# A hybrid attention and pooling block: TensorE keeps to the order of the program's text from attention on

## The chip, the cores and the metric

The kernel runs on one core of a Trainium2 chip. The metric is device time in microseconds (us); three runs of the kernel before gave 1914.45, 1915.05 and 1915.29 us, median 1915.05. The core's engines each work through an instruction stream of their own and wait for each other by semaphores: TensorE (PE) multiplies matrices and transposes, VectorE (DVE), ScalarE (ACT) and GpSimd (POOL) work elementwise, SyncE (SP) issues the transfers. Only PE writes matmul results to PSUM, from which DVE and ACT read them.

## The reference

One layer over 4096 tokens of width 1024, in float32; cut to what matters:

```python
h    = rms_norm(x, norm_g) * (1 + scale) + shift          # scale, shift, gate from c @ w_ada
proj = h @ w_in                                           # 1024 -> 3*512 + 512 + 1024
q = rms_norm(proj[..., :512]  as 8 heads of 64, q_norm_g)
k = rms_norm(proj[..., 512:1024] as 8 heads, k_norm_g)
v, u, z = the rest
# each chunk of 64 tokens attends to itself and 8 chunks to its left
s = einsum('bqhd,bkhd->bhqk', qn, kn) * 64**-0.5 + bias
a_out = einsum('bhqk,bkhd->bqhd', softmax(s), vn)
p_out = (trailing means of u over 2, 4, 8, 16 tokens - u) @ w_pool * pool_scale
y = concat([a_out, p_out]) * silu(z)
x = x + gate * (y @ w_out)
```

## The kernel before

Each product is made of three passes with split operands (high by high, high by low, low by high), so projections come in threes of matmuls (L599 to L601, and likewise L528 to L530, L863 to L865).

The kernel has three stages. The first (to 557 us) normalises x and makes z and u; its matmuls are L330 to L332. The second, attention, is the one that changes first. It runs in two phases `ph` of four heads; in each phase, eight groups `sg` of 512 tokens. A *unit* is one head of one group, 64 units in all, numbered 0 to 63. For one unit:

- Scores: `s1_items`, four steps of 128 queries. Matmuls L697 and L698 write `sps`, of which there is one buffer. DVE (L702) adds the bias and takes the maximum, ACT (L715) takes the exponential and the row sums, into `p`.
- Transposes and values: `s2_items`. For each key block `tr(j)` transposes up to four 128x128 pieces of `p` on PE (L745) into `ptps` (three buffers), ACT casts them (L751, `pth`) and DVE takes the rest (L752, `ptl`); `pv(j)` multiplies both with v (L763, L764) into `ops`. `tr` runs one key block ahead of `pv`. At the end `fin` adds the two halves (ACT L778, DVE L779), and after every second head POOL multiplies the result by the gate and by the reciprocal sums (L781, L782).
- Work beside it: the projection of one 128-token block to q, k and v for a later group (`proj_items`, 24 wide matmuls for q and k, then 24 narrow ones for v), or, in units 58 to 62, the first part of the output projection (`o_items`).

q and k of a block must be normalised before they are transposed. When the wide matmuls of a block end, ACT copies the result (L612), POOL squares it (L614), DVE sums (L621); after every second block a reciprocal root is taken for the two together (L94 to L102: thirteen small operations on POOL and two on DVE), and POOL scales both blocks (L630). The low part of each half of the next h blocks (L111, `bhl`) is made on POOL, too. `tq` then transposes the four blocks of a group (L651), and the copies (L659 to L671) put them where the scores read them.

In the text, unit u is written as one merged list: `merge` spreads the transposes and values of unit u, the scores of unit u+1 and the projection matmuls evenly over the unit. `turns` inserts the q and k transposes of group g into units 4g-2 (two tiles), 4g-1 and 4g, three places into the list of projection work. The block that a group needs last, 4g+3, is projected in unit 4g-3.

That text is not the order that runs. The program is built with a scheduler that plays the program on a simulated timeline and gives each engine whichever instruction is ready first by it. So projection matmuls are moved forward past transposes whose input is late in that timeline. The third stage (`d_items`, from 1695 us) is the rest of the output projection.

Of the kernel before, what the change touches and what calls it, by code (L numbers as in the profile page):

```python
# [23 lines left out]
KT = D // P  # L24
# [27 lines left out]
def block_kernel(ctx, tc, x, xT, par, crow, w_adaT, w_in, w_uT, bias, w_pool, w_out, rcnt, out):  # L52
    nc = tc.nc
# [422 lines left out]
                    load_wqkv(0, 1, lambda: a_stage(), nc.vector)  # L476


    op = ctx.enter_context(tc.tile_pool(name="b_qk", bufs=9))
    WO = {}  # L480

# [37 lines left out]
    def o_items(i):  # L519
        half, p = osteps[i]  # L520

        def one(k):
            if half == 0 and k == 0:
                XP[p] = (pp.tile([P, SG], F32, name="ps"), load_xr(p, 0))
            ps, xr = XP[p]
            a_, l_ = OH[i]
            wh, wl = WO[10 * half][k]
            nc.tensor.matmul(ps, a_[:, k, :], wh, start=half == 0 and k == 0, stop=False, skip_group_check=True)  # L528
            nc.tensor.matmul(ps, a_[:, k, :], wl, start=False, stop=False, skip_group_check=True)
            nc.tensor.matmul(ps, l_[:, k, :], wh, start=False, stop=k == 3, skip_group_check=True)  # L530
            if k == 3:
                OH.pop(i)
                o_load(i + 2)
                o_done(i)
                if half == 0:
                    t = op.tile([P, 512], F32, name="qkr")
                    nc.scalar.copy(t, ps)
                    nc.sync.dma_start(s1_d[p], t)
                else:
                    nc.vector.tensor_tensor(xr, ps, xr, op=ALU.add)  # L540
                    nc.sync.dma_start(out[p * P : (p + 1) * P, 0:512], xr)
                    XP.pop(p)

        return [lambda k=k: one(k) for k in range(4)]

    with ExitStack() as cb:
# [42 lines left out]
        def proj_items(ph, b, after=None):  # L589
# [3 lines left out]
            def chunk(c, k):  # L593
                if k == 0:
                    hold[c] = pp.tile([P, SG], F32, name="ps")
                ps = hold[c][:, 0:512] if c == 0 else hold[c][:, 0:256]
                a_, l_ = hq[(ph, b), k]
                wh, wl = WB[ph, c, k]
                nc.tensor.matmul(ps, a_, wh, start=k == 0, stop=False)  # L599
                nc.tensor.matmul(ps, a_, wl, start=False, stop=False)  # L600
                nc.tensor.matmul(ps, l_, wh, start=False, stop=k == KT - 1)  # L601
                if k == KT - 1:
                    if c == 0:
                        evac_qk(ps)
                    else:
                        evac_v(ps)
                if c == 1 and k in (3, 7) and after is not None:
                    load_h(*after, k // 4, nc.vector if ph == 0 and b < 5 else None)
# [37 lines left out]
        def tq_items(ph, sg):  # L646
            def tq(which, pair):
                ps = ptp.tile([P, SG], F32, name="ptps")
                c0 = which * 256 + pair * P
                for i in range(NB):  # L650
                    nc.tensor.transpose(  # L651
                        out=ps[:, i * P : (i + 1) * P], in_=QK[ph, sg * NB + i][:, c0 : c0 + P], identity=ident
                    )
                for e in range(2):
# [24 lines left out]
        def s1_items(ph, sg, h):  # L679
            def one(i):  # L680
# [13 lines left out]
                ks = ring[h]  # L694
                for pos, k0, n in parts:
                    o = ps[:, pos : pos + n]
                    nc.tensor.matmul(o, QS[ph, sg, h][:, qc], ks[:, k0 : k0 + n], start=True, stop=False)  # L697
                    nc.tensor.matmul(o, QL[ph, sg, h][:, qc], ks[:, k0 : k0 + n], start=False, stop=True)  # L698
                w0 = 0 if sg > 0 else 512 - i * P
                p_ = sp.tile([P, WIN], F32, name="p")  # L700
                mx = st.tile([P, 1], F32, name="mx")
# [32 lines left out]
        def s2_items(ph, sg, h):  # L734
# [5 lines left out]
            def tr(j):  # L740
                ilo, ihi = max(j, 0), min(j + 4, 3)
                ps = ptp.tile([P, SG], F32, name="ptps")
                for i in range(ilo, ihi + 1):
                    w = (j - i + 4) * P
                    nc.tensor.transpose(  # L745
                        out=ps[:, i * P : (i + 1) * P], in_=Pt[ph, sg, h, i][:, w : w + P], identity=ident
                    )
                r = slice(ilo * P, (ihi + 1) * P)
                a_ = wk.tile([P, SG], F32R, name="pth", bufs=3)
                l_ = wk.tile([P, SG], F32R, name="ptl", bufs=3)  # L750
                nc.scalar.copy(a_[:, r], ps[:, r])  # L751
                nc.vector.tensor_tensor(l_[:, r], ps[:, r], a_[:, r].bitcast(F32), op=ALU.subtract)  # L752
                pts[j] = (a_, l_, r)

            def pv(n):
# [4 lines left out]
                a_, l_, r = pts.pop(j)  # L760
                v = Vt[ph, sg * NB + j][:, pr, e, :]
                last = n == len(js) - 1
                nc.tensor.matmul(o[:, r], v, a_[:, r], start=n == 0, stop=False, skip_group_check=True)  # L763
                nc.tensor.matmul(o[:, r], v, l_[:, r], start=False, stop=last, skip_group_check=True)  # L764
                if last:
                    fin(o)

# [76 lines left out]
        def d_items(i):  # L844
            t, p = steps[i]

            def one(k):
# [12 lines left out]
                a_, l_ = DH[t, p]  # L860
                wh, wl = WO[11 if t == 0 else t][k]
                start = t in (1, 2) and k == 0
                nc.tensor.matmul(ps, a_[:, k, :], wh, start=start, stop=False, skip_group_check=True)  # L863
                nc.tensor.matmul(ps, a_[:, k, :], wl, start=False, stop=False, skip_group_check=True)  # L864
                nc.tensor.matmul(ps, l_[:, k, :], wh, start=False, stop=k == 3, skip_group_check=True)  # L865
                if k < 3:
                    return

# [156 lines left out]
```

## Time and profile before

| | us |
|---|---|
| median of three runs | 1915.05 |
| the profiled execution | 1916.19 |
| its span | 1914.3 |
| busy in it: PE | 1876.1 (98%) |
| DVE | 1198.1 (63%) |
| ACT | 914.9 (48%) |
| POOL | 697.7 (36%) |

Busy time is what an engine's instructions cover. Matmuls are pipelined and the ends of their records are modelled and overlap the next record, so short waits hide in a busy PE; the distance from one start to the next shows them. The chain that ended last is PE for 90%.

### The profile page before, as it was taken

How to read it: one execution, taken by the hardware profiler on the slowest of the kernel's cores; microseconds unless marked ns; L12 is line 12 of the kernel's file. 1: busy time of each engine (PE TensorE's matmuls, PEld its weight loads, DVE VectorE, ACT ScalarE, POOL GpSimd, SP SyncE). 2: the span in 40 equal slices, each digit the busy share in tenths (PEclk: the TensorE clock that was granted, in tenths of full speed). 3: DMA queues.
4: the chain of work that ended last, by engine and by line, in shares of the span. 5: the costliest groups of instructions: out<-in, count | busy, mean ns of one | idle time of the engine just before them, and what ended most of it. 6: DMA issues, size and time to landing. Idle time of an engine off the chain costs nothing.

```text
span 1914.3 us, 29736 instructions
## 1 busy us (share of the span) xinstructions
PE 1876.1 (98%) x10284; PEld 1616.1 (84%) x10284; DVE 1198.1 (63%) x2424; ACT 914.9 (48%) x1951; POOL 697.7 (36%) x966
## 2 busy tenths in 40 slices
PE   8999999999999999999999999999999999989999
PEld 7888888888888888888887888988988888878887
DVE  8676666575544457656656665576566555478875
ACT  5422223332324457656657665576566666432221
POOL 0421355244135553444454564534444433200000
PEclk8999999999999999999999999999999999999999
DMA  9566466567222222221223222222212457686662
GB/s 376 192 198 198 151 216 213 185 200 258 75 100 73 72 67 67 65 69 53 60 83 111 78 85 75 69 61 67 67 62 67 181 185 230 234 297 221 208 205 78
DMA packets 196727, 265.63 MB, mean 139 GB/s; under 512 B 21984, under 2 KB 98272, under 8 KB 196576
## 3 DMA queue, kind: packets, MB, share of 16 engines
q1 hardware_dynamic: 196576, 263.73, 42.1%
q8 instruction: 81, 1.33, 0.3%
q14 instruction: 70, 0.57, 0.1%
HBM read 177.54 MB, written 77.74 MB: 133 GB/s over the span
## 4 chain that ended last, share of the span: by engine, by line
PE 90%; DVE 4%; ACT 2%; DMA 2%; issue 1%; SPq 0%; POOL 0%; ACTq 0%; DVEq 0%; POOLq 0%
PE ps L599 9%; PE ps L600 9%; PE ps L601 9%; PE ptps L745 6%; PE aps L330 5%; PE aps L332 5%; PE aps L331 5%; PE ps L330 4%; PE ps L331 4%; PE ps L332 4%; PE sps L697 3%; PE ops L764 3%; PE sps L698 3%; PE ops L763 3%; PE ptps L865 2%; PE ptps L864 2%
## 5 line engine op out<-in xcount | busy, mean ns | idle before, releaser
L599 PE MATMUL ps<-w,bhh 128*128 128x512 f32 (+1 forms) x1024 | 353.9, 346 | 0.8 <-ACT bhh L110 0.8
L600 PE MATMUL ps<-w,bhh 128*128 128x512 f32 (+1 forms) x1024 | 352.3, 344 | 0.4 <-DVE w L111 0.4
L601 PE MATMUL ps<-w,bhl 128*128 128x512 f32 (+1 forms) x1024 | 351.0, 343 | 0.0
L752 DVE TENSOR_TENSOR ptl<-ptps,pth 128x512 fp32r<-128x512 f32 x480 | 223.4, 485 | 157.3 <-ACT pth L751 153.0
L702 DVE CUSTOM_DVE_ANT_0 p<-sps,nb 128x640 f32<-128x640 f32 (+4 forms) x256 | 199.0, 777 | 127.6 <-PE sps L698 126.5
L751 ACT CAST pth<-ptps 128x512 fp32r<-128x512 f32 x480 | 192.5, 425 | 147.1 <-PE ptps L745 123.1
L111 POOL TENSOR_TENSOR bhl<-bhr,bhh 128x512 fp32r<-128x512 f32 x148 | 190.8, 1292 | 157.7 <-ACT bhh L110 123.4
L715 ACT ACTIVATE p<-p,mx 128x640 f32<-128x640 f32 (+4 forms) x256 | 204.5, 799 | 91.0 <-DVE mx L702 88.5
L745 PE MATMUL ptps<-ident,p 128*128 128x128 f32 x1200 | 215.3, 275 | 1.6 <-ACT p L715 1.4
L599 PEld LDWEIGHTS ps<-w,bhh 128*128 128x128 f32 x1024 | 194.2, 190 | 19.0 <-DVE v L111 1.1
L600 PEld LDWEIGHTS ps<-w,bhh 128*128 128x128 f32 x1024 | 194.1, 190 | 18.5 <-DVE w L111 1.1
L601 PEld LDWEIGHTS ps<-w,bhl 128*128 128x128 f32 x1024 | 194.1, 190 | 16.4
L763 PE MATMUL ops<-pth,v 128*128 128x512 f32 x480 | 162.3, 339 | 5.7 <-ACT pth L751 3.5
L745 PEld LDWEIGHTS ptps<-ident,p 128*128 128x128 f32 x1200 | 147.4, 140 | 21.0 <-ACT p L715 1.9
L697 PE MATMUL sps<-kr,qs 128*128 128x320 f32 (+2 forms) x480 | 154.5, 330 | 8.8 <-DVE mx L702 7.3
L764 PE MATMUL ops<-ptl,v 128*128 128x512 f32 x480 | 154.2, 331 | 2.9 <-DVE ptl L752 2.2
L614 POOL TENSOR_TENSOR sq<-qkr 128x512 f32<-128x512 f32 x64 | 66.6, 1041 | 247.1 <-ACT qkr L612 238.6
L331 PE MATMUL aps<-hlo,w 128*128 128x512 f32 x392 | 152.8, 390 | 0.0
L332 PE MATMUL aps<-hhi,w 128*128 128x512 f32 x392 | 152.8, 390 | 0.0
L330 PE MATMUL aps<-hhi,w 128*128 128x512 f32 x392 | 149.6, 392 | 0.0
L698 PE MATMUL sps<-kr,ql 128*128 128x320 f32 (+2 forms) x480 | 147.3, 317 | 0.0
L331 PE MATMUL ps<-hlo,w 128*128 128x512 f32 x376 | 146.6, 390 | 0.0
(202 smaller groups left out, 3932.0 us busy)
## 6 DMA issues: line engine op xcount, KB each, us to landing
bhr<-hT_d SPq DMA_DIRECT2D x128, 256.0 KB
xt<-in_x_dram SPq DMA_DIRECT2D x32, 512.0 KB
qkr<-in_x_dram SPq DMA_DIRECT2D x64, 256.0 KB
out_dram<-qkr SPq DMA_DIRECT2D x64, 256.0 KB
yv<-yT_d SPq DMA_DIRECT2D x61, 256.0 KB
xt<-in_xT_dram SPq DMA_DIRECT2D x28, 512.0 KB
hT_d<-xt SPq DMA_DIRECT2D x56, 256.0 KB
w<-wg_d SPq DMA_DIRECT2D x20, 512.0 KB
```

What stands on the lines that cost most here:

```text
L330: nc.tensor.matmul(ps, wh[:, cs], a_, start=k == 0, stop=False)
L331: nc.tensor.matmul(ps, wh[:, cs], l_, start=False, stop=False)
L332: nc.tensor.matmul(ps, wl[:, cs], a_, start=False, stop=k == KT - 1)
L599: nc.tensor.matmul(ps, a_, wh, start=k == 0, stop=False)
L600: nc.tensor.matmul(ps, a_, wl, start=False, stop=False)
L601: nc.tensor.matmul(ps, l_, wh, start=False, stop=k == KT - 1)
L697: nc.tensor.matmul(o, QS[ph, sg, h][:, qc], ks[:, k0 : k0 + n], start=True, stop=False)
L698: nc.tensor.matmul(o, QL[ph, sg, h][:, qc], ks[:, k0 : k0 + n], start=False, stop=True)
L745: nc.tensor.transpose(out=ps[:, i * P : (i + 1) * P], in_=Pt[ph, sg, h, i][:, w : w + P], identity=ident)
L752: nc.vector.tensor_tensor(l_[:, r], ps[:, r], a_[:, r].bitcast(F32), op=ALU.subtract)
L763: nc.tensor.matmul(o[:, r], v, a_[:, r], start=n == 0, stop=False, skip_group_check=True)
L764: nc.tensor.matmul(o[:, r], v, l_[:, r], start=False, stop=last, skip_group_check=True)
```

## The change

Two helpers wrap every matmul and transpose from attention on. `keep_in_program_order` ties an instruction to the one before it in the text on the same engine, without a semaphore: the scheduler can't move it ahead. The 2465 PE instructions of the first stage stand as before. No operation, operand or buffer changes; the order of the other engines is chosen by the scheduler again, around PE's new order.

```diff
+    def mm(*a, **kw):
+        tc.keep_in_program_order(nc.tensor.matmul(*a, **kw))
+
+    def turn_(**kw):
+        tc.keep_in_program_order(nc.tensor.transpose(**kw))
...
-                nc.tensor.matmul(ps, a_, wh, start=k == 0, stop=False)
-                nc.tensor.matmul(ps, a_, wl, start=False, stop=False)
-                nc.tensor.matmul(ps, l_, wh, start=False, stop=k == KT - 1)
+                mm(ps, a_, wh, start=k == 0, stop=False)
+                mm(ps, a_, wl, start=False, stop=False)
+                mm(ps, l_, wh, start=False, stop=k == KT - 1)
...
-                    nc.tensor.transpose(
+                    turn_(
                         out=ps[:, i * P : (i + 1) * P], in_=QK[ph, sg * NB + i][:, c0 : c0 + P], identity=ident
                     )
...
-                    nc.tensor.matmul(o, QS[ph, sg, h][:, qc], ks[:, k0 : k0 + n], start=True, stop=False)
-                    nc.tensor.matmul(o, QL[ph, sg, h][:, qc], ks[:, k0 : k0 + n], start=False, stop=True)
+                    mm(o, QS[ph, sg, h][:, qc], ks[:, k0 : k0 + n], start=True, stop=False)
+                    mm(o, QL[ph, sg, h][:, qc], ks[:, k0 : k0 + n], start=False, stop=True)
...
-                nc.tensor.transpose(
+                turn_(
                     out=ps[:, i * P : (i + 1) * P], in_=Pt[ph, sg, h, i][:, w : w + P], identity=ident
                 )
...
-                nc.tensor.matmul(o[:, r], v, a_[:, r], start=n == 0, stop=False, skip_group_check=True)
-                nc.tensor.matmul(o[:, r], v, l_[:, r], start=False, stop=last, skip_group_check=True)
+                mm(o[:, r], v, a_[:, r], start=n == 0, stop=False, skip_group_check=True)
+                mm(o[:, r], v, l_[:, r], start=False, stop=last, skip_group_check=True)
```

`o_items` and `d_items` change likewise. Since the helpers record the instructions, all these matmuls now have line L481 and all transposes L484; tiles tell them apart (`sps` scores, `ptps<-ident,p` transposes of p, `ops` values, `ptps<-ident,qkr` transposes of q and k, `ps` projections). Below L478 the lines move down by 7: L614 becomes L621, L630 L637, L781 and L782 become L788 and L789.

First place: PE, the end of a unit and the start of the next, just ahead of the transposes of group 3. Before:

```order
L697 MATMUL sps<-kr_4826,qs_6818 128x512
L698 MATMUL sps<-kr_4826,ql_4830 128x512
L697 MATMUL sps<-kr_4826,qs_6818 128x128
L698 MATMUL sps<-kr_4826,ql_4830 128x128
L599 MATMUL ps<-w,bhh 128x256
L600 MATMUL ps<-w,bhh 128x256
L601 MATMUL ps<-w,bhl 128x256
L599 MATMUL ps<-w,bhh 128x512
L600 MATMUL ps<-w,bhh 128x512
L764 MATMUL ops<-ptl,v 128x256
L745 MATMUL ptps<-ident,p 128x128
```

Now:

```order
L481 MATMUL sps<-kr_4825,ql_4829 128x512
L481 MATMUL ps<-w,bhh 128x256 x2
L481 MATMUL ps<-w,bhl 128x256
L481 MATMUL ops<-pth,v 128x256
L481 MATMUL ops<-ptl,v 128x256
L481 MATMUL ps<-w,bhh 128x256 x2
L481 MATMUL ps<-w,bhl 128x256
L481 MATMUL ops<-pth,v 128x128
L481 MATMUL ops<-ptl,v 128x128
L481 MATMUL ps<-w,bhh 128x512 x2
L481 MATMUL ps<-w,bhl 128x512
L484 MATMUL ptps<-ident,p 128x128 x4
```

The last of the four transposes reads what the scores at the top give through DVE and ACT. Between them stand now always the same few matmuls; before, the scheduler set them apart as it liked, and cut triples and tiles open.

Second place: PE, the first q and k transposes of group 3, a dozen rows on. Before:

```order
L745 MATMUL ptps<-ident,p 128x128 x2
L764 MATMUL ops<-ptl,v 128x128
L745 MATMUL ptps<-ident,p 128x128 x2
L651 MATMUL ptps<-ident,qkr 128x128 x4
L601 MATMUL ps<-w,bhl 128x512
L599 MATMUL ps<-w,bhh 128x512
```

Now:

```order
L481 MATMUL sps<-kr_4826,qs_6818 128x128
L481 MATMUL sps<-kr_4826,ql_4830 128x128
L481 MATMUL ps<-w,bhh 128x512 x2
L481 MATMUL ps<-w,bhl 128x512
L481 MATMUL ops<-pth,v 128x512
L481 MATMUL ops<-ptl,v 128x512
L484 MATMUL ptps<-ident,qkr 128x128 x4
L484 MATMUL ptps<-ident,p 128x128 x3
```

What the rows don't show is where the block that they need last was projected: now between the wide matmuls of block 15 and these four stand 24 narrow and 9 wide projection matmuls with their share of attention; before, the wide matmuls of blocks 15, 16 and on had been moved ahead by several units.

Third place: POOL, the end of the chain from the square of a block's q and k to the scaling of the pair (here block 11, the last of group 2). Before:

```order
L99 TENSOR_TENSOR rqw<-rqy 128x16
L100 TENSOR_TENSOR rqw<-rqw,rqv 128x16
L101 TENSOR_SCALAR rqw<-rqw 128x16
L102 TENSOR_TENSOR rqy<-rqw,rqy 128x16
L630 TENSOR_TENSOR qkr<-qkr,rqy 128x512 x2
L614 TENSOR_TENSOR sq<-qkr 128x512
L111 TENSOR_TENSOR bhl<-bhr,bhh 128x512 x2
L781 TENSOR_TENSOR osum<-osum,gzb 128x512
L782 TENSOR_TENSOR osum<-osum,rlx 128x512
```

Now:

```order
L111 TENSOR_TENSOR bhl<-bhr,bhh 128x512
L101 TENSOR_SCALAR rqw<-rqw 128x16
L102 TENSOR_TENSOR rqy<-rqw,rqy 128x16
L99 TENSOR_TENSOR rqw<-rqy 128x16
L100 TENSOR_TENSOR rqw<-rqw,rqv 128x16
L788 TENSOR_TENSOR osum<-osum,gzb 128x512
L101 TENSOR_SCALAR rqw<-rqw 128x16
L789 TENSOR_TENSOR osum<-osum,rlx 128x512
L102 TENSOR_TENSOR rqy<-rqw,rqy 128x16
L637 TENSOR_TENSOR qkr<-qkr,rqy 128x512 x2
```

The two multiplications of a finished pair of heads (`osum`) stood behind the scaling of q and k and stand now inside the chain to it; two `bhl` are in the chain before and now (of the two, the last is the first row here). That is so in every group's last block but the first's.

## Rows read from the trace of the kernel before

**Rows 1.** The page: span and busy times.
```profile
span 1914.3 us, 29736 instructions
PE 1876.1 (98%) x10284; PEld 1616.1 (84%) x10284; DVE 1198.1 (63%) x2424; ACT 914.9 (48%) x1951; POOL 697.7 (36%) x966
```
**Rows 2.** Windows: stretch; busy (instructions) by engine; granted clock, DMA share, GB/s.
```profile
700.00:750.00 50.00, 46.95 (x292) 40.27 (x291) 35.69 (x88) 35.58 (x84) 17.28 (x29) 1.00 0.18 54
1000.00:1050.00 50.00, 45.35 (x285) 39.09 (x285) 35.16 (x83) 37.39 (x87) 25.88 (x34) 1.00 0.35 107
1704.70:1708.10 3.40, 1.05 (x5) 0.57 (x4) 3.40 (x7) 0.00 (x0) 0.00 (x0) 1.00 1.05 358
1708.10:1711.50 3.40, 3.40 (x9) 2.62 (x9) 3.04 (x6) 0.00 (x0) 0.00 (x0) 0.50 1.04 353
1750.00:1800.00 50.00, 50.00 (x222) 41.43 (x221) 39.49 (x63) 11.22 (x18) 0.00 (x0) 1.00 0.71 231
556.90:1695.50 1138.60, 1115.98 (x6871) 985.07 (x6871) 679.05 (x1583) 687.89 (x1568) 517.72 (x793) 1.00 0.31 100
```
**Rows 3.** Lines by form, PE, 556.9 to 1695.5: count, busy, mean ns, idle before.
```profile
L745 PE MATMUL ptps<-ident,p 128*128 128x128 f32 x1200 | 215.3, 275 | 1.6 <-ACT p L715 1.4
L599 PE MATMUL ps<-w,bhh 128*128 128x512 f32 x512 | 205.6, 402 | 0.8 <-ACT bhh L110 0.8
...
L599 PE MATMUL ps<-w,bhh 128*128 128x256 f32 x512 | 148.3, 290 | 0.0
L697 PE MATMUL sps<-kr,qs 128*128 128x320 f32 x256 | 81.8, 327 | 4.5 <-DVE mx L702 3.5
```
**Rows 4.** Timeline of PE near 802 us: start, duration, instruction.
```profile
801.38 0.28 PE L601 MATMUL ps<-w,bhl 128*128 128x256 f32 x1
801.50 0.34 PE L763 MATMUL ops<-pth,v 128*128 128x384 f32 x1
...
802.66 0.38 PE L745 MATMUL ptps<-ident,p 128*128 128x128 f32 x2
...
803.00 0.28 PE L601 MATMUL ps<-w,bhl 128*128 128x256 f32 x1
```
**Rows 5.** Timeline, block 19: last wide matmul, square and scaling on POOL.
```profile
797.34 0.48 PE L601 MATMUL ps<-w,bhl 128*128 128x512 f32 x1
...
798.62 1.04 POOL L614 TENSOR_TENSOR sq<-qkr 128x512 f32<-128x512 f32 x1 [3.56 <-ACT qkr L612]
...
807.90 2.04 POOL L630 TENSOR_TENSOR qkr<-qkr,rqy 128x512 f32<-128x512 f32 x2
```
**Rows 6.** Timeline of POOL, block 3, with nothing else in the chain.
```profile
588.88 1.04 POOL L614 TENSOR_TENSOR sq<-qkr 128x512 f32<-128x512 f32 x1 [6.63 <-ACT qkr L612]
...
596.21 2.05 POOL L630 TENSOR_TENSOR qkr<-qkr,rqy 128x512 f32<-128x512 f32 x2
```
**Rows 7.** Lines by form, POOL, attention.
```profile
L781 POOL TENSOR_TENSOR osum<-osum,gzb 128x512 f32<-128x512 f32 x32 | 41.5, 1296 | 125.4 <-DVE osum L779 120.6 <-PE ps L529 2.8 <-issue 1.7
```
**Rows 8.** Timeline near 1686 us: scores, exponential, and the transpose that waits for it.
```profile
1684.80 0.31 PE L698 MATMUL sps<-kr,ql 128*128 128x320 f32 x1
...
1686.50 0.83 ACT L715 ACTIVATE p<-p,mx 128x640 f32<-128x640 f32 x1
...
1687.47 0.44 PE L745 MATMUL ptps<-ident,p 128*128 128x128 f32 x2 [1.19 <-ACT p L715]
```
**Rows 9.** Lines by form, attention: DVE's and ACT's steps of scores and transposes.
```profile
L702 DVE CUSTOM_DVE_ANT_0 p<-sps,nb 128x640 f32<-128x640 f32 x224 | 183.5, 819 | 109.5 <-PE sps L698 108.6
L752 DVE TENSOR_TENSOR ptl<-ptps,pth 128x512 fp32r<-128x512 f32 x120 | 79.4, 683 | 40.7 <-ACT pth L751 39.8
...
L751 ACT CAST pth<-ptps 128x512 fp32r<-128x512 f32 x120 | 66.3, 586 | 34.5 <-PE ptps L745 33.0 <-PE ops L764 0.3
```
**Rows 10.** Timeline of PE: two waits.
```profile
1653.88 0.51 PE L528 MATMUL ps<-w,bhh 128*128 128x512 f32 x1 [1.97 <-ACT bhh L110]
...
1707.59 0.50 PE L863 MATMUL ps<-w,bhh 128*128 128x512 f32 x1 [2.35 <-DVE qkr L870]
```

More of the change, by code (lines that the diff above doesn't have):

```diff
@@ L527, in one @@
             wh, wl = WO[10 * half][k]
-            nc.tensor.matmul(ps, a_[:, k, :], wh, start=half == 0 and k == 0, stop=False, skip_group_check=True)
-            nc.tensor.matmul(ps, a_[:, k, :], wl, start=False, stop=False, skip_group_check=True)
-            nc.tensor.matmul(ps, l_[:, k, :], wh, start=False, stop=k == 3, skip_group_check=True)
+            mm(ps, a_[:, k, :], wh, start=half == 0 and k == 0, stop=False, skip_group_check=True)
+            mm(ps, a_[:, k, :], wl, start=False, stop=False, skip_group_check=True)
+            mm(ps, l_[:, k, :], wh, start=False, stop=k == 3, skip_group_check=True)
             if k == 3:
@@ L862, in one @@
                 start = t in (1, 2) and k == 0
-                nc.tensor.matmul(ps, a_[:, k, :], wh, start=start, stop=False, skip_group_check=True)
-                nc.tensor.matmul(ps, a_[:, k, :], wl, start=False, stop=False, skip_group_check=True)
-                nc.tensor.matmul(ps, l_[:, k, :], wh, start=False, stop=k == 3, skip_group_check=True)
+                mm(ps, a_[:, k, :], wh, start=start, stop=False, skip_group_check=True)
+                mm(ps, a_[:, k, :], wl, start=False, stop=False, skip_group_check=True)
+                mm(ps, l_[:, k, :], wh, start=False, stop=k == 3, skip_group_check=True)
                 if k < 3:
```

## The prediction

> **What bounds the kernel now.** I read the page first: PE is busy for 98% of the span [rows 1], DVE, ACT and POOL for 63, 48 and 36%, so on the face of it PE sets the time and has 38 us to give. That is too small, since the records of matmuls overlap. So I went on to the timeline of PE, for the distance from one start to the next where nothing waits. In the last stage 222 matmuls of 512 columns start in 50 us [rows 2], 0.225 us each. One of 256 columns is followed after 0.12 us; two transposes and one such matmul fill 802.66 to 803.00, so a transpose takes (0.34 - 0.12)/2 = 0.11 [rows 4]. On the straight line through the two sizes, 384, 320 and 128 columns take 0.173, 0.146 and 0.068.
>
> Then the counts, by form, for the attention stretch of 1138.6 us with its 6871 PE instructions [rows 2, 3]. Of 512 columns: 3 x 512 in the projection, 240 in the values (two for each of 120 tiles [rows 9]), 112 in the scores, 384 in the output projection and 38 at the end, 2310 x 0.225 = 520 us. Of 256: 3 x 512 + 240 + 112 = 1888 x 0.12 = 227. Of 320: 2 x 256 = 512 x 0.146 = 75. Of 384 and 128: 352 each, 61 and 24. Transposes: 1200 of p and 256 of q and k, 160. Together 1067 us. So PE loses **72 us** in attention, most of it in pieces too small to be called idle; the windows from 700 and from 1000 us, where only 46.95 and 45.35 us of 50 are covered, are two of the worse stretches [rows 2]. In the first PE has little projection left to run, because the order of before spent it early; the second lies between the phases. 72 us is what a better order could give at most, and the text's order changes only where the losses lie.
>
> **The change, part by part.** No operation is added or removed, so the 1067 us stay; what I work out is the waits in the text's order, each as a time that a result needs less the PE work that now stands in between. Where the next reader is PE itself, everything queued behind it on PE waits along, that is the whole kernel.
>
> *Transposes of q and k (groups 1 to 15).* From the end of block 4g+3's wide matmuls to the fourth q and k transpose stand 24 narrow (2.88 us) and 9 wide projection matmuls (2.03), 15 transposes (1.65), 12 score matmuls (1.75) and 12 value matmuls of all sizes (1.55): 9.9 us. Taken from the modelled end of the last wide matmul it is 9.7, as the record ends 0.16 later than its step. In that time ACT and POOL must copy, square, take the root and scale. In block 19 this ran from 797.82 to 809.94: 12.1 us [rows 5], with two `bhl` inside. With nothing else inside, in block 3, it took 9.4 from the square on (598.26 - 588.88) [rows 6], and with the 0.8 ahead of the square in block 19 (797.82 to 798.62) 10.2. The new order of POOL puts the two `osum` multiplications into it as well, 2 x 1.30 us [rows 7]: 14.7. They will hardly wait themselves: by the same prices the unit's values end 5.4 us after the wide matmuls, copy and addition are done by about 8, and POOL reaches them at 8 to 9. Before PE arrives, it has itself waited about 1.0 us for scores and transposes (next paragraphs). So 14.7 - 10.7 = 4.0 us for each of eleven groups, 44 us. Groups 1 and 9 lie behind shorter units (first transposed pieces only), 7.6 + 1.0 us: 6.1 each, 12. Group 7 has four more splits of new weights in the chain (17.3 - 8.6 = 8.7), group 15 stands at 9.6 (5.1), group 0 has the short chain against 8.8 (1.4). Sum **71 us**. Bounds: without `osum` in the chain and with PE late by 1 us it is 12.1 - 10.7 = 1.4 a group, 30 us in all with the special ones; if the copies or the splits queue for two more us, 100. I take 71, since the order says what is in the chain and rows have each duration.
>
> Before, this wait costs nothing: no row of PE names POOL's scaling, because the wide matmuls of that block ran 28 us of PE work or more ahead.
>
> *Scores to the first transposes of the next unit.* From the last score to the transpose of its piece stand six narrow matmuls (0.72), in every second unit three wide ones as well (0.68), four value matmuls (0.38) and three transposes (0.33): 1.43 and 2.1 us by turns. What it takes, once: the scores' last matmul starts at 1684.80 and is through 0.15 later, ACT's exponential follows at 1686.50, the transpose starts at 1687.47: 2.5 us [rows 8]. The floor, with no queue, is 0.2 to DVE, 0.82 + 0.08 there [rows 9], 0.83 and 0.19 on ACT and 0.1 between them: some 2.05, an estimate from these rows. With 2.5: 1.1 and 0.4 by turns, 0.75 on the mean, for 48 ordinary units 36 us, 0.7 for the eight units of each phase's first group and a bit for the first: **43 us**. At the floor only the odd half waits, 0.6 x 28 = 18; with a mean of 2.8, 60.
>
> *Transposes to values.* ACT's cast and DVE's rest of a full tile take 0.59 + 0.68 [rows 9], 1.6 us with handing over, against 2.4 to 3.4 us of PE work; the last two tiles of a unit, smaller, have 1.1 and 0.9 against 2.0 and 1.6. All are covered unless an exponential or a scaling is in front (0.7 to 0.8 us), as it sometimes will be with DVE 60% and ACT 60% busy (679 and 688 of 1139 us [rows 2]). I take half a collision of 0.8 us per unit: 48 x 0.4 = **19 us**, between 0 and 40.
>
> *The clock.* Behind a wait of 1.97 us at 1651.9 the granted clock stayed at full rate; behind one of 2.35 us at 1705.2 [rows 10] it was 0.50 for the next 3.4 us, 1.2 of 2.4 GHz [rows 2], and nine matmuls started where fifteen fit: 1.4 us lost. A wait of 4 us is longer than either. I take 15 groups x 1.4 with four in five struck, **17 us**; between 0 and 35, as a long wait might cost twice.
>
> *Between the phases, and the end.* Units 26 and 27 have no projection until the second phase's weights are there. Before, the window from 1000 us holds most of that loss; now those units run bare, with the transposes' full 1.6 us against about 1: 10 us. The last unit has the same lack, 5 us. **15 us**, between 10 and 25. The start of the last stage stays as it is.
>
> **Sum.** 71 + 43 + 19 + 17 + 15 = 165 in place of 72: +93 us. The profiled execution took 1916.2 us (its span of 1914.3 and 1.9 around it), which gives 2009; it lies 1.1 above the median of the runs, so **2008 us**.
>
> **The rivals.**
> 1. *The text's even spread pays.* The bare stretches of before fill up, and PE loses only the 15 us between phases and at the end: 1915 - 72 + 15 = 1858. The place is the q and k transposes: it decides from the point where POOL's chain fits into 9.7 us. For it speaks that the distances from transposes to values are all longer than the unqueued times; against it that even the chain without any neighbour took 10.2 [rows 5, 6]. 5%.
> 2. *As much lost as before.* All waits lie at their floors, 30 + 18 + 0 + 0 + 20 = 68: 1911 to 1915. It needs POOL to be done with `osum` beforehand, and empty queues. 4%.
> 3. *Short waits take the clock, too.* Behind the wait of 2.35 us it fell [rows 2, 10]; if each unit's wait for its exponential did the same, 56 x 1.4 = 78 us would come on top, 2086 us. Against it: the window from 700 us has the most waits of its neighbourhood and was granted 1.00 [rows 2]. 6%. The Trainium skill says in "TensorE: Matmul & The Clock Gate", section "A second HAM failure mode: psum-queue depth-cycling", that frequent micro-idles between groups of matmuls made the clock swing between half and full rate. By that rule the time would be this rival's; the trace has not shown it for waits up to 1.97 us.
> 4. *The pins don't bind.* Then nothing moves, 1915. The order of PE shows otherwise: triples stand together from the first matmul of attention to the last. Under 1%.
>
> **How the numbers follow.** Slower by several per cent, as summed: 83%; rival 1 5%, rival 2 4%, rival 3 6%, something else slower 2%. The likeliest is the sum, 2008. Its own range follows from the bounds: the four terms of 30 to 100, 18 to 60, 0 to 40 and 0 to 35 are not at one end all together; half of their joint spread is some 45 us either way, 1963 to 2053. With rivals 1 and 2 below and 3 above left out, 1960 to 2056 holds about 8 in 10. A measurement of this kernel can tell 0.2% (4 us) from no change: slower 92%, within it 2%, faster 6%.
>
> **What would show it.** In the profile after: PE's waits at the transposes of q and k (`ptps<-ident,qkr`) name POOL's `qkr` scaling, some fifteen times with 3 to 5 us each, and the chain of waits goes over POOL; transposes of p wait for ACT's `p` in most units, near 1 us in every second; short stretches at granted clock 0.50 lie behind the long waits; PE's busy share falls to about 93%, with the first stage to 557 us unchanged. I am wrong if POOL's scaling is seldom named, if the waits of the q and k transposes sum to under 30 us, or if the rest of PE's waits alone make up more than 100.

## The result and the profile after

The changed kernel took 2036.94 us (median of 4 runs, 2034.40 to 2040.01), against 1915.17 for the kernel before beside it: a ratio of 1.0635, 95% interval 1.0622 to 1.0649. Forecast were 2008 us, between 1960 and 2056. The profiled execution took 2040.01 us. Its page, span and busy times:

```profile
span 2038.2 us, 29831 instructions
PE 1911.2 (94%) x10284; PEld 1632.9 (80%) x10284; DVE 1218.1 (60%) x2424; ACT 916.5 (45%) x1951; POOL 695.8 (34%) x966
```

Against [rows 1] the span is 124 us longer and POOL's and ACT's work the same to 2 us (DVE's is 20 longer for as many instructions): nothing was added, PE stands still longer. The windows (columns as in [rows 2]):

```profile
1050.00:1100.00 50.00, 33.52 (x196) 28.49 (x195) 26.25 (x59) 28.80 (x64) 23.89 (x31) 0.86 0.35 102
557.90:1817.90 1260.00, 1148.16 (x6869) 999.20 (x6867) 700.56 (x1582) 689.04 (x1567) 514.59 (x793) 0.98 0.29 90
```

All of the difference lies in attention: 1260 us in place of 1138.6 [rows 2], for the same 6870 instructions. The place between the phases, one of the worse stretches before, is now the worst of attention: only 33.52 of 50 us are covered. The granted clock is no longer 1.00 throughout.

The waits of PE by what ended them (us in all, times, the longest):

```profile
PE ptps L484 <- POOL qkr L637: 53.2, 32, 9.0
PE ptps L484 <- ACT p L722: 27.9, 31, 1.4
PE ops L481 <- DVE ptl L759: 12.7, 31, 1.5
PE ps L481 <- DVE qkr L547: 10.1, 12, 1.5
```

The first is the one that no row of before had: two waits in each of 16 groups, for POOL's scaling of q and k. The first two of a group's transposes read a pair of blocks that was scaled earlier; the third and the fourth read the last pair. Here is one of them, group 4, which needs block 19 (as [rows 5]); the timeline of PE and POOL from the last wide matmul of that block:

```profile
849.00 0.39 PE L481 MATMUL ps<-w,bhl 128*128 128x512 f32 x1
...
858.31 1.30 POOL L788 TENSOR_TENSOR osum<-osum,gzb 128x512 f32<-128x512 f32 x1
...
859.74 1.27 POOL L789 TENSOR_TENSOR osum<-osum,rlx 128x512 f32<-128x512 f32 x1
...
861.27 2.04 POOL L637 TENSOR_TENSOR qkr<-qkr,rqy 128x512 f32<-128x512 f32 x2
```

```profile
859.99 0.38 PE L484 MATMUL ptps<-ident,qkr 128*128 128x128 f32 x2
862.37 0.33 PE L484 MATMUL ptps<-ident,qkr 128*128 128x128 f32 x1 [1.99 <-POOL qkr L637]
863.37 0.33 PE L484 MATMUL ptps<-ident,qkr 128*128 128x128 f32 x1 [0.67 <-POOL qkr L637]
```

From the end of the wide matmuls (849.39) to the end of the scaling (863.31) it is 13.9 us, with both `osum` multiplications inside. PE has its first two transposes at 859.99, 10.6 after, and then starts the third 2.4 and the fourth 3.4 us after that. Behind it, windows around two such places, groups 4 and 3:

```profile
860.70:864.10 3.40, 1.06 (x7) 0.83 (x8) 0.00 (x0) 0.50 (x3) 2.53 (x4) 1.00 0.48 149
864.10:867.50 3.40, 3.40 (x11) 2.63 (x10) 1.97 (x3) 1.36 (x3) 0.00 (x0) 0.51 0.28 66
793.00:796.40 3.40, 3.40 (x18) 2.87 (x19) 2.04 (x4) 2.10 (x4) 0.00 (x0) 1.00 0.19 43
```

After group 4 PE ran at 1.2 GHz for 3.4 us; after group 3, where the two waits were 1.24 and 0.67, it stayed at 2.4.

**The account.** For all kernels I took the start of each PE instruction in attention and subtracted, from the distance to the one before, what this pair of shapes takes where nothing waits (close to the prediction's prices [rows 2, 4]; the kernel before comes to 69.9 us by it, not 72). What is left is lost time, put down to the instruction that started late; the total also holds the many steps that are late by less than 0.04. The last column is the length of the stretches at 1.2 GHz in attention.

| | time | q, k transposes | p transposes | values | scores and projections | total lost | at 1.2 GHz |
|---|---|---|---|---|---|---|---|
| before | 1915 | 0.6 | 8.4 | 19.4 | 28.6 | 69.9 | 0 |
| after | 2036.9 | 62.5 | 39.5 | 29.8 | 52.4 | 191.9 | 61 |
| e1 late turns | 2016.4 | 13.4 | 65.2 | 35.3 | 49.6 | 171.4 | 27 |
| e2 early scores | 2046.1 | 81.1 | 7.3 | 45.0 | 59.9 | 201.3 | 92 |
| e3 `osum` on DVE | 2002.7 | 33.9 | 37.0 | 29.8 | 48.2 | 156.8 | 34 |
| e4 lead of two | 2065.6 | 86.1 | 54.2 | 8.4 | 59.5 | 216.4 | 99 |
| c1 = e1 + e2 | 1978.9 | 15.0 | 11.1 | 57.0 | 41.8 | 133.7 | 20 |
| c2 = e1 + e2 + e4 | 1934.4 | 16.1 | 5.5 | 13.9 | 41.6 | 85.7 | 14 |
| p1 projection pinned only | 1929.1 | 4.6 | 11.6 | 17.0 | 44.6 | 85.4 | 31 |
| p2 projection free | 1972.1 | 2.5 | 23.0 | 43.6 | 47.7 | 126.2 | 3 |
| f1 = c2, output free | 1921.4 | 16.7 | 5.9 | 15.8 | 27.0 | 73.6 | 24 |
| f2 = f1, splits on DVE | 1912.6 | 7.1 | 6.7 | 15.2 | 27.1 | 64.6 | 10 |
| f3 c2's text, no pin | 1925.4 | 0.5 | 15.4 | 19.8 | 31.7 | 75.6 | 0 |
| f4 before, splits on DVE | 1915.4 | 1.1 | 9.2 | 21.2 | 28.5 | 69.2 | 3 |

From 69.9 to 191.9 is 122 us, and the time grew by 121.8. That must be so where the same instructions stand at the same prices; what the account adds is the place. Half of the growth, 62 us, lies at the transposes of q and k, 31 at those of p, 10 at the values and 24 in scores and projections (the small steps, which only the total holds, lose 5 less).

### The profile page after: what moved, and what is told of

Its sections match the earlier page's. It is cut to its first block, busy times and chain, and to the rows that moved or that the text cites. A ratio compares the mean times of both kernels' runs of the same rounds, so it can differ in the third digit from the quotient of the medians.

```text
span 2038.2 us, 29831 instructions
## 1 busy us (share of the span) xinstructions
PE 1911.2 (94%) x10284; PEld 1632.9 (80%) x10284; DVE 1218.1 (60%) x2424; ACT 916.5 (45%) x1951; POOL 695.8 (34%) x966
## 5 line engine op out<-in xcount | busy, mean ns | idle before, releaser
L481 PE MATMUL ps<-w,bhh 128*128 128x512 f32 (+1 forms) x2568 | 729.7, 368 | 12.8 <-DVE qkr L547 10.1
L481 PEld LDWEIGHTS ps<-w,bhh 128*128 128x128 f32 x2568 | 433.8, 193 | 48.5 <-DVE qkr L547 15.1
L481 PE MATMUL ps<-w,bhl 128*128 128x512 f32 (+1 forms) x1284 | 452.7, 353 | 0.0
L759 DVE TENSOR_TENSOR ptl<-ptps,pth 128x512 fp32r<-128x512 f32 x480 | 233.0, 489 | 261.0 <-ACT pth L758 258.7
L758 ACT CAST pth<-ptps 128x512 fp32r<-128x512 f32 x480 | 199.6, 422 | 168.6 <-PE ptps L484 164.4
L481 PEld LDWEIGHTS ps<-w,bhl 128*128 128x128 f32 x1284 | 245.0, 191 | 33.9
L484 PE MATMUL ptps<-ident,p 128*128 128x128 f32 x1200 | 220.9, 278 | 28.1 <-ACT p L722 27.9
L484 PEld LDWEIGHTS ptps<-ident,p 128*128 128x128 f32 x1200 | 157.0, 142 | 73.2 <-ACT p L722 37.3
L621 POOL TENSOR_TENSOR sq<-qkr 128x512 f32<-128x512 f32 x64 | 66.6, 1041 | 401.6 <-ACT qkr L619 400.3
L481 PE MATMUL ops<-ptl,v 128*128 128x512 f32 x480 | 161.1, 336 | 14.0 <-DVE ptl L759 12.7
L481 PE MATMUL sps<-kr,qs 128*128 128x320 f32 (+2 forms) x480 | 155.0, 332 | 2.7 <-DVE mx L709 2.7
L481 PE MATMUL ops<-pth,v 128*128 128x512 f32 x480 | 155.3, 324 | 1.7 <-ACT pth L758 1.7
L332 PE MATMUL ps<-hhi,w 128*128 128x512 f32 x376 | 146.9, 391 | 0.0
L481 PE MATMUL sps<-kr,ql 128*128 128x320 f32 (+2 forms) x480 | 146.7, 317 | 0.0
L330 PE MATMUL ps<-hhi,w 128*128 128x512 f32 x376 | 146.4, 393 | 0.0
```

The lines of the kernel that those rows point to most:

```text
L330: nc.tensor.matmul(ps, wh[:, cs], a_, start=k == 0, stop=False)
L332: nc.tensor.matmul(ps, wl[:, cs], a_, start=False, stop=k == KT - 1)
L481: tc.keep_in_program_order(nc.tensor.matmul(*a, **kw))
L484: tc.keep_in_program_order(nc.tensor.transpose(**kw))
L621: nc.gpsimd.tensor_tensor(sq, raw, raw, op=ALU.mult)
```

## The experiments

For e1 to e4, theory A was that the losses are separate distances in the text, each too short for its chain, so that an edit brings most of what it takes away. Rival R was that DVE and ACT set the pace and a wait that goes comes back as another (for e3, rival P: the place of `osum` doesn't matter). Only e3 came out at theory A's figure. So from c1 on theory A is another one: in each group the wait for POOL's chain binds, and other savings count only once it is covered. The edits below are against the changed kernel. "Ordinary" groups are 2 to 6 and 10 to 14; the others stand at the start, the change or the end of a phase.

**e1, late turns.** The q and k transposes are put later into the list of each unit's projection work.

```diff
-                work.insert(min(len(work), 3 + 6 * n), f)
+                work.insert(min(len(work), 9 + 5 * n), f)
```

> The changed kernel with the q and k transposes six places later in the list of projection work (text only; PE still pinned). By the same step prices the last of the four transposes then stands 15.7 us behind the block's wide matmuls in ordinary groups, 12.3 in groups 1 and 9, 9.9 in group 7, against POOL's chain of 14.0 (20.0 in group 7). Theory A (the losses are separate distances, each too short for its chain): PE's 53 us of waits named POOL's scaling fall under 15, the half-rate stretches outside the change of phase go, other waits grow by 5 to 10 us; 1970 to 1985 us against 2037. Rival R (in this rhythm DVE and ACT set the pace, a wait that goes comes back as another): the other waits grow by what POOL's give up; 2020 us or more.

Measured: 2016.43 us, ratio to before 1.0528 [1.0511, 1.0544], between the two and nearer to rival R's 2020. PE's waits:

```profile
PE ptps L484 <- ACT p L722: 43.9, 37, 1.9
...
PE ptps L484 <- POOL qkr L637: 9.1, 7, 6.0
```

POOL's wait is gone but for the groups that are not ordinary (53.2 to 9.1): in ordinary groups the third transpose now stands 16.9 us or more behind the wide matmuls, and the chain still takes 14.0. But PE waits 16 us more for the exponential, and loses 26 more at the transposes of p in the account, where theory A had other waits grow by 5 to 10. The timeline shows where this comes from:

```profile
869.89 0.31 PE L481 MATMUL sps<-kr,ql 128*128 128x320 f32 x1
869.95 0.74 DVE L678 SCALAR_TENSOR_TENSOR kr<-ptps,pt,kr 64x512 fp32r<-64x512 f32 x1
...
870.94 0.81 DVE L709 CUSTOM_DVE_ANT_0 p<-sps,nb 128x640 f32<-128x640 f32 x1
...
872.09 0.62 ACT L110 CAST bhh<-bhr 128x512 fp32r<-128x512 f32 x1
...
872.90 0.83 ACT L722 ACTIVATE p<-p,mx 128x640 f32<-128x640 f32 x1
...
873.87 0.48 PE L484 MATMUL ptps<-ident,p 128*128 128x128 f32 x1 [1.73 <-ACT p L722]
```

The copies of the transposed q and k, which now come later too, stand on DVE in front of the last scores' bias, and on ACT, with a copy and two casts behind them, in front of the exponential: 3.8 us from score to transpose where [rows 8] has 2.5. So moving the transposes takes the wait away and makes another.

**e2, early scores.** The scores of the next unit are spread over one step more, so that the last stands earlier in the unit.

```diff
-            s1 = s1_items(*units[u + 1]) if u + 1 < 64 else []
+            s1 = s1_items(*units[u + 1]) + [none] if u + 1 < 64 else []
```

> The changed kernel with the four score steps of a unit spread as if there were five, the last place empty: from the last scores to the next unit's first transposes 2.9 and 3.6 us of PE work in place of 1.4 and 2.1, while the last transposes to their values fall from 1.9 and 1.5 to 1.3 and 1.0. Theory A: PE's 28 us of waits named ACT's exponential fall under 5, those named DVE's ptl grow from 13 by 10 to 15, and PE arrives earlier at the q and k transposes, so POOL's waits grow by about 9; 2020 to 2030 us. Rival R: no gain at all, 2035 us or more.

Measured: 2046.09 us, 1.0679 [1.0662, 1.0697]: slower than the changed kernel, as rival R has it, though the wait it aims at is gone.

```profile
PE ptps L484 <- POOL qkr L637: 71.2, 32, 9.6
PE ops L481 <- DVE ptl L759: 20.9, 41, 1.7
...
PE ptps L484 <- ACT p L722: 0.6, 1, 0.6
```

In the account PE loses 32 us less at the transposes of p, but 19 more at those of q and k, 15 more at the values, whose transposes now stand nearer to them, and 8 more in scores and projections. The longer waits bring more time at 1.2 GHz, 92 us for 61.

The 19 us at the q and k transposes have two sources. PE comes there 0.2 or 0.8 us sooner by turns, which is 5 us over all groups. And POOL's chain itself has grown, from 13.9 or 14.0 us to 15.0 or 15.1 in ordinary groups, 13 us over all groups. Group 4 again, from the last wide matmul:

```profile
849.25 0.39 PE L481 MATMUL ps<-w,bhl 128*128 128x512 f32 x1
...
853.56 1.28 POOL L111 TENSOR_TENSOR bhl<-bhr,bhh 128x512 fp32r<-128x512 f32 x1 [0.70 <-ACT bhh L110]
...
856.66 1.29 POOL L111 TENSOR_TENSOR bhl<-bhr,bhh 128x512 fp32r<-128x512 f32 x1 [0.59 <-ACT bhh L110]
...
862.62 2.04 POOL L637 TENSOR_TENSOR qkr<-qkr,rqy 128x512 f32<-128x512 f32 x2
```

POOL stands idle in front of both `bhl`, until ACT has cast their blocks; after the change it was idle before neither. So most of PE's longer wait for POOL comes from a longer chain; the smaller part is time that PE had saved on its way there.

**e3, `osum` on DVE.** The two multiplications leave POOL's chain.

```diff
-                    nc.gpsimd.tensor_tensor(Ot[pr], Ot[pr], hold["g"], op=ALU.mult)
-                    nc.gpsimd.tensor_tensor(Ot[pr], Ot[pr], rlb[pr], op=ALU.mult)
+                    nc.vector.tensor_tensor(Ot[pr], Ot[pr], hold["g"], op=ALU.mult)
+                    nc.vector.tensor_tensor(Ot[pr], Ot[pr], rlb[pr], op=ALU.mult)
```

> The changed kernel with the two osum multiplications on DVE in place of POOL, so that POOL's chain to the scaling loses 2 x 1.3 us and ends some 11.4 us after the wide matmuls in place of 14.0. Theory A: POOL's waits fall from 53 to some 20 (a floor of 0.9 a group stays, as the two blocks of a pair are scaled one after the other), half-rate stretches become fewer, DVE's additional 1.4 us in every second unit costs 5; about 2000 us, 1992 to 2012. Rival P (the place of osum in the chain does not matter, since POOL had to wait for something else there): POOL's waits stay over 45 us, 2030 us or more.

Measured: 2002.73 us, 1.0458 [1.0442, 1.0473], 34 us below the changed kernel.

```profile
PE ptps L484 <- POOL qkr L637: 26.9, 22, 3.7
PE ptps L484 <- ACT p L722: 26.7, 30, 1.4
```

The chain took 12.1 to 12.7 us in ordinary groups (13.9 to 14.0 after), POOL's waits halved, the others stayed, and half of the time at 1.2 GHz went too. A shorter chain pays in full: over all groups it is 27 us shorter, and 29 us less are lost at the q and k transposes.

**e4, a lead of two.** Transposes run two key blocks ahead of the values.

```diff
-LOOK = 1
+LOOK = 2
```

> The changed kernel with the transposes two key blocks ahead of the values in place of one: the last tiles get 2.6 and 2.0 us of PE work in place of 1.9 and 1.5, the others 3.1 or more. Theory A: the waits of the value matmuls for DVE's and ACT's halves (14 us named, some 25 by the starts) nearly go, the waits for the exponential stay; 2010 to 2022 us. Rival R: the same time comes back at the transposes, 2032 us or more.

Measured: 2065.59 us, 1.0785 [1.0769, 1.0801], the slowest of all, where theory A had a gain.

```profile
PE ptps L484 <- POOL qkr L637: 74.6, 32, 9.1
PE ptps L484 <- ACT p L722: 35.8, 55, 1.3
...
PE ops L481 <- DVE ptl L759: 0.6, 1, 0.6
```

The values' wait is gone, and POOL's wait takes 21 us more (24 in the account). Of these 24, 9 are from PE coming sooner, by 0.55 or 1.15 us in ordinary groups, and 13 from a chain that takes 15.0 or 15.1 us here, too. POOL is idle in it for 2.5 us in group 4, where after the change it was 1.5:

```profile
858.05 1.29 POOL L111 TENSOR_TENSOR bhl<-bhr,bhh 128x512 fp32r<-128x512 f32 x1 [1.54 <-ACT bhh L110]
...
860.58 0.22 POOL L99 TENSOR_TENSOR rqw<-rqy 128x16 f32<-128x16 f32 x1 [0.95 <-DVE rqy L96]
```

With 8 us more of waits for the exponential (15 in the account), since transposes that stand earlier need their exponential earlier, it is a loss.

**c1 and c2, the edits together.** c1 has e1's and e2's, c2 e4's as well.

> Both edits tried singly before, together: the q and k transposes stand later in a unit's list (9+5n places in place of 3+6n), and the scores of the next unit are through one step earlier. Theory A (each group has one binding wait, POOL's chain; only when that is covered do other savings count): the wait of the q and k transposes stays near 10 us, and now the earlier scores pay what they could not pay alone, the transposes of p fall from 65 us (late transposes alone) to some 20: about 1970 us. Rival R (DVE and ACT set the pace, and the waits come back elsewhere): 2000 us or more.

> The same two edits and transposes two key blocks ahead of the values in place of one. Each of the last two edits alone made the kernel slower. Theory A: with POOL's chain covered the values' wait (35 us) falls to some 10 as well, and the time to 1935 to 1955 us. Rival R: the same 2000 us or more as without it, since DVE and ACT then only queue elsewhere.

Measured: c1 1978.85 us, 1.0329 [1.0314, 1.0344]; c2 1934.40 us, 1.0100 [1.0082, 1.0118]. Waits of c1, then of c2:

```profile
PE ops L481 <- DVE ptl L759: 22.0, 50, 0.9
PE ops L481 <- ACT pth L758: 13.7, 19, 2.2
```

```profile
PE ps L481 <- DVE qkr L547: 13.6, 14, 2.1
PE ptps L484 <- POOL qkr L637: 12.5, 6, 9.7
PE ops L481 <- DVE ptl L759: 6.3, 7, 1.1
```

With POOL's wait out of the way, the earlier scores that had cost 9 us alone bring 38 (2016.4 to 1978.9), and the lead of two that had cost 29 alone brings 44. For the earlier scores two things had changed: the q and k transposes lose no more by them (2 us in place of 19), and there was more to save at the transposes of p, since e1 had raised that loss to 65 (it falls by 54 us, not by 32). c1 came out 9 us above the figure of theory A, with the loss at the values grown to 57; c2 lies just below A's range. In c2 the third and fourth q and k transposes of ordinary groups start 16.7 us or more behind the wide matmuls, and the chain took 14.4 to 14.5: nothing waits.

**p1 and p2, half of the change each.** p1 pins only the projection's matmuls (L606 to L608), p2 pins all but them.

```diff
-                mm(ps, a_, wh, start=k == 0, stop=False)
-                mm(ps, a_, wl, start=False, stop=False)
-                mm(ps, l_, wh, start=False, stop=k == KT - 1)
+                nc.tensor.matmul(ps, a_, wh, start=k == 0, stop=False)
+                nc.tensor.matmul(ps, a_, wl, start=False, stop=False)
+                nc.tensor.matmul(ps, l_, wh, start=False, stop=k == KT - 1)
```

(p2; in p1 these three are pinned and all other matmuls and transposes are free.)

> Only the projection's matmuls keep the text's order among each other; transposes, scores, values and output projection are the scheduler's again. If it is the projection held back to the text's even spread that costs, because the last block of a group is then projected too late, some of the loss stays: in its order 15.5 us of PE work stand between a block's wide matmuls and the transposes (10.7 in the changed kernel, 28 or more before), which covers POOL's chain of 14: 1930 to 1980 us. If the projection's place doesn't matter at all, 1915; if it is all of the loss, 2037.

> The mirror image: everything keeps the text's order except the projection's matmuls, which the scheduler may move forward. Then the last block of a group is projected 50 us and more ahead of its transposes, as before, and the scheduler can put projection matmuls behind the scores. Theory A: no wait for POOL's chain, the other waits mostly filled, 1915 to 1935 us. Rival: if pinning transposes, scores and values in itself costs (the waits for ACT and DVE, 70 us), about 1975 us.

Measured: p1 1929.14 us, 1.0067 [1.0050, 1.0084], just under my range; p2 1972.10 us, 1.0296 [1.0280, 1.0311]. For p2 my theory was wrong, and its rival right. Waits of p1, then of p2:

```profile
PE sps L481 <- DMA qs<-qs: 14.4, 12, 1.6
```

```profile
PE ops L481 <- DVE ptl L759: 16.9, 36, 1.5
...
PE sps L481 <- DVE mx L709: 9.4, 38, 0.7
PE ptps L484 <- ACT p L722: 8.9, 14, 1.7
```

In p2 the projection runs ahead as before (its q and k transposes stand 53 us or more behind their wide matmuls in groups 2 to 15) and no wait for POOL is left. Beyond what the kernel before loses, it loses 24 us at the values, 15 at the transposes of p and 19 in scores and projections, of which some 10 are a wait in the output projection's first part (below). My reading is that the bare stretches behind the projection now lie among transposes and values that can't close up; no run takes this apart. In p1 the projection holds still and the scheduler sets the third and fourth q and k transposes later, to 15.7 us or more behind the wide matmuls in ordinary groups, so POOL's chain of 14.1 to 14.2 is covered; PE's largest wait there is of scores for the transfer of `qs`, 14.4 us. Alone, the halves cost 13 and 56 us (against 1916.27 for the kernel before beside them), and both together cost 122: some 53 us exist only when neither side may move.

**f1 to f4, the rest of c2.** f1 is c2 with the matmuls of the output projection's first part (L535 to L537, `o_items`) free; f2 is f1 with one line more; f3 is the kernel before with c2's three edits and no pin; f4 is the kernel before with f2's line.

```diff
-                load_wqkv(1, 0, stage, nc.gpsimd)
+                load_wqkv(1, 0, stage, nc.vector)
```

> Late q and k transposes, early scores and two key blocks of lead as in the run before, and in the output projection's first part (units 58 to 62) the matmuls are the scheduler's again. What this part waits for (DVE's L547, 13.6 us, in 14 waits, since the next step takes the buffer that the last one has just filled) should go, at the price of bare units behind it: theory A (each wait is a matter of what PE has left to put in between) 1921 to 1930 us. Rival: the scheduler runs this projection ahead in one piece, as its order shows, and the last units lose what it saves: 1934 us or more.

> The same, and the low parts of the second phase's first weights are made on DVE, not on POOL. They stand in POOL's chain of group 7, where 23.7 us ran against 12.9 to 14 of PE work and PE waited for 9.7. Theory A (the chain's length is what PE waits for): the chain falls to 13 to 15, the wait to under 2, 8 us less than without it and some 2 of the clock: 1912 to 1922 us, level with the kernel before. Rival: DVE, with eight more splits of 0.7, is late for scores and transposes there instead: no gain.

> The kernel before with the three edits of the text alone (late q and k transposes, early scores, two key blocks of lead) and nothing pinned, the scheduler chooses. It tells whether the text's better order or the pin brings the 1934. Theory A: the scheduler moves the projection ahead again and undoes most of it, 1905 to 1930 us. Rival: the better text helps the scheduler too, under 1900 us.

> The kernel before with one edit: the low parts of the second phase's first weights are made on DVE, not on POOL, as in the run before, which came out just ahead of the kernel before. It tells what that version owes to this edit. Theory A (the edit pays only where PE waits for POOL's chain of group 7, and before, PE doesn't): no change, 1912 to 1919 us. Rival: POOL or the weights' readiness matters to the kernel before as well, 1905 to 1911 us.

Measured: f1 1921.41 us, 1.0033 [1.0020, 1.0046]; f2 1912.64, 0.9987 [0.9977, 0.9996]; f3 1925.35, 1.0054 [1.0038, 1.0071]; f4 1915.37, 0.9997 [0.9988, 1.0006]. POOL's wait in f1, then in f2:

```profile
PE ptps L484 <- POOL qkr L637: 12.7, 6, 9.9
```

```profile
PE ptps L484 <- POOL qkr L637: 2.3, 4, 0.7
```

All four came out within the ranges of their theory A. Without the splits group 7's chain falls from 24.1 (f1) to 15.2 us, the wait of 9.9 goes, and the time falls by 9. The same line in the kernel before does nothing, since PE doesn't wait there. So the text's order, pinned but for the output projection's first part, is level with the kernel before when the text leaves POOL's chain and the exponential room: 3 us less, where the interval excludes no change, if barely. Without the pin the same text is 10 us slower than before.

## Why the prediction was right, and where its sum was not

The direction and the mechanism are as forecast: no work is added, PE waits in the text's order for POOL's scaling at the q and k transposes of each group, and this is the largest term. The time lies 29 us above the forecast; the terms in turn, forecast against the account:

- *Transposes of q and k, 71:* 62.5. The chain took 13.9 to 14.0 us where I had 14.7. Without the wait the fourth transpose would have stood at 10.9, near the 10.7 worked out, or at 11.75 in every second group. Ordinary groups lost 3.05 and 2.3 by turns, not 4.0; group 1 lost 5.4 (6.1 forecast), group 9 the same, group 15 3.4 (5.1), group 0 3.25 (1.4), group 8 6.5. Group 7 lost 11.0 where I had 8.7: six splits of new weights, not four, stood inside its chain of 20.1 us, and both `osum` multiplications, which I had left out there. Here is its wait, between the phases:

```profile
1075.95 0.38 PE L484 MATMUL ptps<-ident,qkr 128*128 128x128 f32 x2
1085.31 0.47 PE L484 MATMUL ptps<-ident,qkr 128*128 128x128 f32 x1 [8.98 <-POOL qkr L637]
```

- *Scores to the next unit's transposes, 43:* 39.5. ACT's `p` ended 31 waits of PE, the longest 1.4 us. They are 0.9 us on the mean, near the 1 us that I had for every second unit, but they come in half of the units, not in most.
- *Transposes to values, 19:* 29.8. DVE's `ptl` ended 31 waits, so there was a collision at every second unit, and at some places more than 0.8 us.
- *The clock, 17:* small steps late within the stretches at 1.2 GHz add up to 21 us. It fell for 61 us in 12 stretches, 11 of them behind the q and k transposes of a group, near the four groups in five of the forecast, though not by chance: groups 2, 4, 6, 10, 12 and 14, with waits of 1.99 and 0.67 us, were struck each time, and groups 3, 5, 11 and 13, with 1.24 and 0.67, never. Four stretches are 7 to 10 us long. (These 21 us are contained in the other columns of the table.)
- *Between the phases and the end, 15:* the stretch from 1050 to 1100 us alone lost 22, of which group 7's wait is counted above. The bare units' term can't be told apart in the account.
- *What I had not:* 10 us in the output projection's first part, where in the text's order each step takes the buffer that DVE's L547 has yet to read; the scheduler had set other work in between, and f1 sets it free (c2 to f1: 13 us). And about 26 us, outside the stretches at 1.2 GHz, of steps that are late by 0.03 to 0.12 us each, many behind a matmul of 128 columns; the kernel before has some 18 us of them too, within its 70. The timeline shows one such pair, first a pair of narrow matmuls behind one of 384 columns, then one behind 128:

```profile
801.33 0.40 PE L481 MATMUL ps<-w,bhh 128*128 128x256 f32 x2
801.56 0.28 PE L481 MATMUL ps<-w,bhl 128*128 128x256 f32 x1
...
802.32 0.28 PE L481 MATMUL ops<-ptl,v 128*128 128x128 f32 x1
802.44 0.45 PE L481 MATMUL ps<-w,bhh 128*128 128x256 f32 x2
802.73 0.29 PE L481 MATMUL ps<-w,bhl 128*128 128x256 f32 x1
```

The two take 0.23 us in the first place and 0.29 in the second. What holds the second up I did not test.

The step that was mis-sized is thus the list of terms: two were missing (10 and some 26 us), the values were 11 short, and the largest was 9 too high. (The terms overlap, so these don't add up to the 27 us between 165 and 191.9.) A further assumption failed without harm to the sum: I priced the waits as independent terms, with a chain of fixed length. e2 and e4 show that they aren't. They took away most of the terms that I had priced at 43 and 19 us, and the kernel became slower by 9 and 29, where theory A had both faster: PE came sooner to POOL's wait, POOL's chain became longer by 1.1 us, and the values or the exponential lost their room.

The rivals: POOL's chain did not fit (rivals 1 and 2 fall), the pins bind (4). Rival 3, the clock taken by the short waits for the exponential as well, did not come: no stretch at 1.2 GHz but one at the change of phase lies elsewhere than behind the q and k transposes. But in e1, where the wait for the exponential grew to 1.73 us, this was the granted clock around it:

```profile
870.20:873.60 3.40, 1.73 (x13) 1.34 (x12) 3.16 (x7) 2.75 (x5) 0.81 (x1) 1.00 0.25 80
873.60:877.00 3.40, 3.13 (x10) 2.64 (x11) 1.25 (x4) 1.39 (x5) 0.46 (x1) 0.50 0.25 83
```

So the clock fell behind a wait for ACT as well as behind one for POOL. The Trainium skill tells in "TensorE: Matmul & The Clock Gate", section "A second HAM failure mode: psum-queue depth-cycling", of a kernel in which frequent micro-idles between groups of matmuls made the clock swing. The traces here agree in part: a fall followed the waits above, but none followed the 31 waits of up to 1.4 us for `p` after the change, nor the single one of 1.97 us before [rows 10].

Of the signs that I had named, PE's busy share is 94% (93 forecast), attention starts at 557.9 us, and the waits for POOL sum to 53 us, above the 30 at which I had called myself wrong; they come as two for each group, not one of 3 to 5. On the last sign, the rest of PE's waits above 100 us, the two measures differ. PE's other idle time in attention is 59 us (1260 less 1148.16 and 53.2), so by that measure the sign did not come. By the account it did: 129 us of the 191.9 are lost elsewhere than at the q and k transposes (the kernel before loses 69 there). So POOL's chain is the largest single cause and half of the growth, not most of the loss. The chain of work that ended last, in the profile, breaks off in the third stage and says nothing of POOL.

## What to carry to other kernels

An engine that takes its work in a fixed order pays each wait whose cover in the text is shorter than the chain behind it: count the work that stands between a result's producer and its reader, and the other engines' chain between them with all that is queued inside it. Such waits are not independent. An edit that saves time ahead of one lets the engine arrive sooner and wait longer, and it shifts the queues of the other engines, so that the chain itself can grow; in e2 and e4 that was the larger part (13 of 19 and 13 of 24 us). So mend the longest wait first, and measure its chain again after each edit: the same edits pay once that wait is covered (c1, c2). A scheduler's freedom can stand in for a text that leaves too little room (the kernel before, 1915), and a text with enough room hardly needs the scheduler (f2, 1913). Half of the freedom in the tight text lay between (p1, 1929, and p2, 1972, against 2037 with none).

## What the runs showed of the hardware that I had not expected

Two waits of 1.99 and 0.67 us, a microsecond apart, were followed by 3.4 us at 1.2 GHz, two of 1.24 and 0.67 by none; in the kernel before, a single wait of 1.97 was not [rows 10]. In e1 a single one of 1.73, with short idle times ahead of it, was. So the length of one wait alone doesn't decide; what else does I did not test. The price differs much between orders of the same work: e4 stood at 1.2 GHz for 99 us of attention, f2 for 10.
